# A two-block transformer on one core: TensorE's share of the background tasks tied to program order, longer pauses in two tasks, and the expert stage's first splits in another order

## The chip, the core and the metric

The kernel runs on one core of a Trainium2 chip. Five engines work side by side and synchronise by semaphores: TensorE (PE, matmuls; its weight loads are listed as PEld), VectorE (DVE), ScalarE (ACT), GpSimd (POOL) and SyncE (SP, which here only issues DMAs). Each engine runs its own instructions strictly in the order in which the program was laid out for it. The metric is the device time of one execution in microseconds (us); the median of the three runs of the kernel before is 2098.64 us.

## What is computed

The input is 256 tokens of 1024 channels. The first block is RMSNorm, a projection, three branches (windowed attention, a bidirectional gated linear recurrence after a short convolution, attention over a memory of 256 rows), a gated merge, and then a feed-forward over 16384 experts: every token scores 2 x 128 sub-keys in each of 8 heads, takes the top 16 of each half, combines them to 256 candidates, takes the top 16 again, and sums gate x gelu(u . h) x v over the chosen experts. Two more layers follow, each with four branches (retention, a convolution of 31 taps, a spatial gating unit, local attention with 8 heads in 2 groups over blocks of 128), a gated merge and a feed-forward.

```python
sc = jnp.einsum('bshpc,hpkc->bshpk', q, sub_keys)
top_v, top_i = lax.top_k(sc, PEER_TOPK)
...
best_v, best_pos = lax.top_k(cand_v, PEER_TOPK)
gate = jax.nn.softmax(best_v, axis=-1)
...
act = jax.nn.gelu(jnp.einsum('chkd,cd->chk', u_tab[ix], hx))
return jnp.einsum('chk,chkd->cd', gx * act, v_tab[ix])
```

The kernel does not gather. It multiplies all 16384 experts in 128 blocks of 128 ("u-blocks"), builds a dense gate for every token and expert from one-hot vectors, multiplies the two, and runs all of v as a second dense matmul.

## The kernel before, in words

**Weights as one stream.** All weights lie in DRAM as 5416 blocks of 128x128 in the order of their use. `Stream.blks` (line 101) hands out one block after the other; every eighth call opens a slot (`_slot`, line 77): ACT copies 128x1024 raw values into a rounded half `whi` (line 91), then DVE or POOL forms the rest `wlo` (line 94; POOL only during the expert projection and the top-k, where `pool_share` is (1, 1)). There are three slots (`SLOT_BUFS`), so ACT can be at most three slots of eight blocks ahead of PE. A matmul of fp32 quality is three matmuls (`mm3`, lines 172 to 176: whi with the high half of the activations, whi with the low half, wlo with the high half); `mm3a` (lines 178 to 182) does the same with 512 columns.

**Background tasks.** What lies between the large projections (attention, convolutions, top-k, the gates' one-hots) is written as generators. `add` (line 144) queues one, `tick` (line 154) is called once for every two weight blocks, and a task that yields n is resumed n x unit ticks later (unit is 4, but 1 for the top-k and the gates). `_step` (line 148) resumes a task, `finish` (line 164) runs it to its end at once. So the pauses are written in weight blocks, that is, in PE's main work.

**Who sets the order.** The program is written in one order, and a scheduler then lays out each engine's instructions (`TileContext(nc, schedule_with_timeline_sim=True)`). It follows the written order as priority, but takes another instruction first where its own timing model says that the first one's operands aren't there yet; so an instruction may stand earlier or later than it was written. The slots' instructions are written under `high_priority` and run ahead as far as their buffers allow. `with tc.issue_after(ins):` ties every instruction written inside, as far as it is on the engine of `ins`, to come after `ins`; the kernel has `ws.on_scalar` and `ws.on_vector`, the last `whi` on ACT and the last `wlo` on DVE.

**The expert stage** (`peer`, line 744). `topk` (line 932) adds the task `picks` (line 1021), then projects the queries (12 column blocks of 8 weight blocks each). `picks` runs eight units (`unit`, line 942), one for each pair of heads and each half of the tokens: PE scores (line 946), then DVE alone does top-16, candidates, top-16 again and index arithmetic with one-hots (lines 1056 to 1063, 953 to 989). A unit is started every `TK_PACE` = 22 ticks, but not before its queries exist. After the last one `yield TK_LAST` (20 ticks), then `gates` (line 991) for both halves, whose softmax has an exponential on ACT (line 997) between DVE's lines 996 and 998 to 1000; 6 ticks later `turn` (line 1004) transposes indices and gates on PE. Meanwhile `u_while` (line 771) multiplies u-blocks as long as the task lives. After that `build` (line 789) makes the gates of experts 0 to 63 of each row in 32 steps (`onehots` on DVE, lines 801 to 806; `products` on PE, ACT and DVE, lines 814 to 831), one step every 8 ticks, again under u-blocks. U-blocks that were made while their place was taken are merged afterwards by multiplications of 128x1024 (lines 853 to 857). A second `build` for experts 64 to 127 (`more`, one step every 10 ticks) is queued, the accumulators are taken, and the loop over v starts: eight weight blocks for each b, u-blocks that are still missing after every odd b, and `weighted` (line 862), which splits the product of gate and activation for b + 1 into `ga` on ACT and DVE (lines 187, 188). At b = 64 the task `more` must be finished (line 865). From block `done` on, `weighted` also has a DVE multiplication (line 868).

**Local attention** (`swa` in `mixers`, line 1221) has four groups in a layer. A group scores on PE (`pss`, line 1230), makes a softmax on DVE and ACT that ends with a multiplication on DVE (line 1247), pauses 3 (12 ticks), transposes on PE (`ptt`, line 244 called from 1255), pauses 1, and multiplies by v (line 1261). The groups are queued at distances of 3 (line 1295). The scores lie in `T4` tiles, of which a layer has 13; the tap convolution (line 1135) runs on DVE beside it, tied to `ws.on_vector`.

Of the kernel before, what the change touches and what calls it, by code (L numbers as in the profile page):

```python
# [7 lines left out]
F32 = mybir.dt.float32  # L8
# [4 lines left out]
AF = mybir.ActivationFunctionType  # L13
ALU = mybir.AluOpType
# [5 lines left out]
P = 128  # L20
S = 256
# [7 lines left out]
N_HA = 96  # L29
HALF = 64  # L30
TK_PACE = 22
TK_LAST = 20
T_OH = 8
PACE = {0: 7.5, HALF: 10}
G_SCALE = 4096.0
# [1 line left out]
NBLK = 128  # L37
# [6 lines left out]
N_BLOCKS = 5416  # L44
W_SHAPE = (-(-N_BLOCKS // 16), 128, 2048)
TAPS = 2
N_SCR = 5
LRU_PACE = 5
N_WARM = 50
# [81 lines left out]
class Core:  # L131
# [14 lines left out]
        return self.tasks[-1]  # L146

    def _step(self, t):
        try:
            t[1] = next(t[0]) * t[2]  # L150
        except StopIteration:
            self.tasks.remove(t)

    def tick(self):
        if self.ticking:
# [16 lines left out]
    def mm3(self, out, wh, wl, xh, xl, start, stop):  # L172
        mm = self.nc.tensor.matmul
        mm(out, lhsT=wh, rhs=xh, start=start, stop=False)  # L174
        mm(out, lhsT=wh, rhs=xl, start=False, stop=False)  # L175
        mm(out, lhsT=wl, rhs=xh, start=False, stop=stop)  # L176

    def mm3a(self, out, wh, wl, xh, xl, start, stop):
        mm = self.nc.tensor.matmul
        mm(out, lhsT=xh, rhs=wh, start=start, stop=False)  # L180
        mm(out, lhsT=xl, rhs=wh, start=False, stop=False)
        mm(out, lhsT=xh, rhs=wl, start=False, stop=stop)  # L182

    def split(self, hi, lo, src, scale=None, eng=None):
        nc = self.nc
# [177 lines left out]
    def build(self):  # L363
        tc, nc, a = self.tc, self.nc, self.a
        with ExitStack() as st:
            cp = st.enter_context(tc.tile_pool(name="cp", bufs=1))
            wp = st.enter_context(tc.tile_pool(name="wp", bufs=1))
            self.tp = st.enter_context(tc.tile_pool(name="tp", bufs=2))
            self.dr = st.enter_context(tc.tile_pool(name="dr", bufs=1, space=DRAM))
            self.cp = cp  # L370
            self.mm = st.enter_context(tc.tile_pool(name="mm", bufs=4, space=PSUM))
            self.bg = st.enter_context(tc.tile_pool(name="bg", bufs=4, space=PSUM))
            self.x = cp.tile([P, KD, S], F32, tag="x", name="x")
            self.par = cp.tile([P, P1_COLS + 2 * KD], F32, tag="par", name="par")
            self.cst = cp.tile([P, C_COLS], F32, tag="cst", name="cst")
            self.ws = Stream(self, wp, a["w"])
            with tc.high_priority(offset=2 * PRIO):
                nc.scalar.dma_start(out=self.par, in_=a["par1"])
                for k in range(0, KD, 2):
                    nc.sync.dma_start(out=self.x[:, k:k + 2, :], in_=a["xT"][:, k:k + 2, :])  # L380
                    if k < 4:
                        self.ws.first(4 * k)
                nc.scalar.dma_start(out=self.cst, in_=a["cst"])
            self.ident = self.cst[:, C_ID:C_ID + P]
            self.hh = cp.tile([P, KD, S], F32R, tag="hh", name="hh")
            self.hl = cp.tile([P, KD, S], F32R, tag="hl", name="hl")
            self.ones = cp.tile([P, 1], F32, tag="ones", name="ones")
            nc.vector.memset(self.ones, 1.0)
            self.eps = cp.tile([P, 1], F32, tag="eps", name="eps")
            nc.vector.memset(self.eps, EPS)  # L390
            self.sqrt_soon(self.eps)
            self.warm()
            self.block1()
            self.peer()
            for l in range(2):
                self.mixers(l)
                self.ffn(l)
# [346 lines left out]
    def peer(self):  # L744
# [4 lines left out]
        tc, nc, a, ws = self.tc, self.nc, self.a, self.ws  # L749
        with ExitStack() as st:  # L750
# [7 lines left out]
            ha = p.tile([P, N_HA, S], F32, tag="ha", name="ha")  # L758
            hb = None

            def h(b):
                return ha[:, b, :] if b < N_HA else hb[:, b - N_HA, :]
# [18 lines left out]
            with tc.tile_pool(name="peg", bufs=1) as gp:  # L781
# [63 lines left out]

                early = ahead
                u_while(self.add(build(0, early), unit=1), HALF + early, early)
                done = ahead
                assert done >= HALF

                cut = NBLK - N_HA
                for b0 in range(early, HALF, 4):
                    for b, k0, k1 in ((ha, b0, min(b0 + 4, HALF, cut)), (hb, max(b0, cut), min(b0 + 4, HALF))):
                        if k0 < k1:
                            o = HALF if b is ha else HALF - N_HA
                            nc.vector.tensor_tensor(out=ha[:, k0:k1, :], in0=ha[:, k0:k1, :],
                                                    in1=b[:, k0 + o:k1 + o, :], op=ALU.mult)
                more = self.add(build(HALF, done), unit=1)
                acc = [pool.tile([P, 2, S], F32, tag=t, name="acc")
                       for pool, t in ((self.mm, "mm"), (self.bg, "bg")) for _ in range(2)]  # L860

                def weighted(b, g):

                    if b == HALF:
                        self.finish(more)
                    src = h(b)
                    if b >= done:
                        nc.vector.tensor_tensor(out=src, in0=src, in1=h(b - done), op=ALU.mult)
                    self.split(g[:, 0, :], g[:, 1, :], src)
                    return g  # L870

                def v_cols(c, b, g, first, last):

# [1 line left out]
                    self.mm3(acc[c // 2][:, c % 2, :], wh, wl, g[:, 0, :], g[:, 1, :],  # L875
                             first and c % 2 == 0, last and c % 2 == 1)

                nxt = weighted(0, ga[0])
                for b in range(NBLK - LAST):
                    cur = nxt  # L880
                    if b + 1 < NBLK - LAST:
# [50 lines left out]
    def topk(self, tp, i1, i2, gt, iot):  # L932
# [58 lines left out]
        def gates(t):  # L991

            bv = bvs[t].rearrange("p (h k) -> p h k", k=16)
            e = tp.tile([P, 8, 16], F32, tag="ge", name="ge")
            sm = tp.tile([P, 2, 8], F32, tag="gs", name="gs")
            nc.vector.tensor_tensor(out=e, in0=bv, in1=bv[:, :, 0:1].to_broadcast([P, 8, 16]), op=ALU.subtract)
            nc.scalar.activation(out=e, in_=e, func=AF.Exp)
            nc.vector.tensor_reduce(out=sm[:, 0, :], in_=e, axis=AX.X, op=ALU.add)
            nc.vector.reciprocal(out=sm[:, 1, :], in_=sm[:, 0, :])
            nc.vector.scalar_tensor_tensor(out=slg[t].rearrange("p (h k) -> p h k", k=16), in0=e, scalar=G_SCALE,  # L1000
                                           in1=sm[:, 1, :, None].to_broadcast([P, 8, 16]),
                                           op0=ALU.mult, op1=ALU.mult)
# [63 lines left out]
    def mixers(self, l):  # L1066
        tc, nc, a, ws = self.tc, self.nc, self.a, self.ws
        with ExitStack() as st:
# [152 lines left out]
            def swa(n, g):  # L1221
# [19 lines left out]
                for i in range(4):  # L1241
# [4 lines left out]
                nc.vector.reciprocal(out=sm[:, 3, :], in_=sm[:, 1, :])  # L1246
                nc.vector.tensor_tensor(out=s[:, :, :nk], in0=s[:, :, :nk],
                                        in1=sm[:, 3, :, None].to_broadcast([P, 4, nk]), op=ALU.mult)
                yield 3
                nkb = nk // P  # L1250
                pts = []
                for kb in range(nkb):
# [39 lines left out]
            self.finish(*loads[1])  # L1292
            self.proj_b(W2["rq"](l), 2, KD, hh, hl, ev_rot(rq))
            self.finish(*t_qk, *loads[0])
            t_swa = [self.add(swa(n, g), 1 + 3 * (2 * n + g)) for n in range(2) for g in range(2)]
            self.proj_b(W2["rq"](l), 4, KD, hh, hl, ev_rot(rq), c0=2)
            self.proj_b(W2["rk"](l), 4, KD, hh, hl, ev_rot(rk))
            rv = T4().rearrange("p a b -> p (a b)").rearrange("p (t c) -> p t c", t=2)
# [326 lines left out]
```

## Time and profile before

| what | value |
|---|---|
| median of three runs | 2098.64 us (2097.73 to 2099.84) |
| the profiled execution's own time | 2103.45 us |
| its span, first to last instruction | 2101.7 us |
| mean granted TensorE clock | 0.986 |
| busy: PE, PEld, DVE, ACT, POOL | 2026.5, 1969.1, 1681.7, 1164.1, 254.8 us |
| instructions | 41465 |

The busy time of PE is 96% of the span, so the table alone says little; what matters is where PE stands, for whom, and at what clock it goes on afterwards. The page cuts the span into 40 slices of 52.5 us and gives each engine's busy share there in tenths. A list of waits sums, for each engine and line, how long it stood and which instruction released it. A timeline lists instructions with start, duration and, in brackets, the idle time before them. A table of stretches gives busy time, number of instructions, and the granted clock of TensorE (1.00 is 2.4 GHz, 0.50 is 1.2 GHz).

### The profile page before, as it was taken

The page shows a single profiled execution, that of the slowest core. Times are in us where ns is not written, and L with a number is a line of the kernel's source. Part 1 is how long each engine was busy: PE and PEld are TensorE (multiplying, and loading weights), DVE is VectorE, ACT ScalarE, POOL GpSimd, SP SyncE. Part 2 cuts the span into 40 slices and gives each one's busy share as a digit, 9 for nine tenths or more (in the row PEclk, how much of TensorE's full clock was granted, in tenths as well). Part 3 has the DMA queues.
Part 4 walks back from the last instruction along what each step waited for, and adds up shares of the span by engine and source line. Part 5 has one row for each costly group of instructions (what it writes and reads, how often), then busy time and mean ns, then how long its engine had stood idle before and what let it go on. Part 6 is the DMA issues. An engine that isn't in the chain of part 4 may idle for free.

```text
span 2101.7 us, 41465 instructions
## 1 busy us (share of the span) xinstructions
PE 2026.5 (96%) x16818; PEld 1969.1 (94%) x16818; DVE 1681.7 (80%) x3308; ACT 1164.1 (55%) x1910; POOL 254.8 (12%) x162
## 2 busy tenths in 40 slices
PE   8999999959999999999999989999999989999999
PEld 7989999959999999999999879999999979999997
DVE  7877779998999999995557989977555999977554
ACT  6688654435555455545546656466455656466443
POOL 2202208741000000000000101200000101200000
PEclk9999999979999999999999999999999999999999
DMA  5444554425454444445554633555555643554554
GB/s 210 141 131 167 209 207 181 161 100 182 181 177 169 157 167 175 172 159 193 201 187 175 219 140 140 182 188 194 193 190 199 219 161 121 201 184 180 193 187 150
DMA packets 57019, 370.01 MB, mean 176 GB/s; under 512 B 6587, under 2 KB 10236, under 8 KB 13564
## 3 DMA queue, kind: packets, MB, share of 16 engines
q1 hardware_dynamic: 50256, 357.06, 47.3%
q10 hardware_dynamic: 6572, 10.31, 1.7%
q8 instruction: 131, 2.15, 0.4%
q14 instruction: 60, 0.49, 0.1%
HBM read 364.73 MB, written 2.62 MB: 175 GB/s over the span
## 4 chain that ended last, share of the span: by engine, by line
PE 82%; DVE 8%; ACT 4%; issue 3%; DMA 2%; POOL 1%; ACTq 0%; SPq 0%; POOLq 0%; DVEq 0%
PE mm L176 6%; PE mm L175 6%; PE mm L174 6%; PE acc L175 6%; PE acc L174 5%; PE acc L176 5%; PE pu L174 5%; PE pu L175 5%; PE pu L176 5%; PE pg L176 3%; PE pg L174 3%; PE pg L175 3%; DVE wlo L94 2%; PE mm L182 2%; PE mm L180 2%
## 5 line engine op out<-in xcount | busy, mean ns | idle before, releaser
L91 ACT ACTIVATE whi<-raw 128x1024 fp32r<-128x1024 f32 x677 | 717.3, 1061 | 765.6 <-PE acc L175 173.5
L94 DVE TENSOR_TENSOR wlo<-raw,whi 128x1024 fp32r<-128x1024 f32 x629 | 779.3, 1239 | 319.5 <-ACT whi L91 314.4
L174 PE MATMUL pu<-hh,whi 128*128 128x256 f32 x1024 | 289.9, 283 | 22.8 <-ACT whi L91 22.8
L176 PE MATMUL mm<-hh,wlo 128*128 128x256 f32 x1008 | 282.8, 281 | 7.4 <-DVE wlo L94 7.4
L176 PE MATMUL pu<-hh,wlo 128*128 128x256 f32 x1024 | 286.7, 280 | 3.0 <-POOL wlo L94 3.0
L175 PE MATMUL pu<-hl,whi 128*128 128x256 f32 x1024 | 285.7, 279 | 0.0
L174 PE MATMUL mm<-hh,whi 128*128 128x256 f32 x1008 | 283.1, 281 | 0.0
L175 PE MATMUL mm<-hl,whi 128*128 128x256 f32 x1008 | 282.0, 280 | 0.0
L175 PE MATMUL acc<-ga,whi 128*128 128x256 f32 x1000 | 268.1, 280 | 3.9 <-DVE ga L188 3.9
L176 PE MATMUL acc<-ga,wlo 128*128 128x256 f32 x1000 | 267.6, 279 | 0.0
L174 PE MATMUL acc<-ga,whi 128*128 128x256 f32 x1000 | 242.3, 281 | 5.0 <-ACT ga L187 5.0
L174 PEld LDWEIGHTS pu<-hh,whi 128*128 128x128 f32 x1024 | 194.3, 190 | 23.0 <-ACT whi L91 23.0
L176 PEld LDWEIGHTS mm<-hh,wlo 128*128 128x128 f32 x1008 | 190.8, 189 | 10.3 <-DVE wlo L94 9.7
L174 PE MATMUL pg<-hh,whi 128*128 128x256 f32 x704 | 197.7, 281 | 0.7 <-ACT gth L618 0.7
L176 PE MATMUL pg<-hh,wlo 128*128 128x256 f32 x704 | 196.9, 280 | 1.1 <-DVE wlo L94 1.1
L176 PEld LDWEIGHTS pu<-hh,wlo 128*128 128x128 f32 x1024 | 193.9, 189 | 3.8 <-POOL wlo L94 3.7
L175 PE MATMUL pg<-hl,whi 128*128 128x256 f32 x704 | 196.1, 279 | 0.0
L175 PEld LDWEIGHTS pu<-hl,whi 128*128 128x128 f32 x1024 | 193.9, 189 | 0.0
L175 PEld LDWEIGHTS mm<-hl,whi 128*128 128x128 f32 x1008 | 192.0, 190 | 1.5 <-issue 1.3
L175 PEld LDWEIGHTS acc<-ga,whi 128*128 128x128 f32 x1000 | 188.8, 189 | 4.6 <-DVE ga L188 4.5
L174 PEld LDWEIGHTS mm<-hh,whi 128*128 128x128 f32 x1008 | 190.9, 189 | 1.0 <-issue 0.7
L176 PEld LDWEIGHTS acc<-ga,wlo 128*128 128x128 f32 x1000 | 188.7, 189 | 0.0
(412 smaller groups left out, 4866.2 us busy)
## 6 DMA issues: line engine op xcount, KB each, us to landing
raw<-in_w SPq DMA_DIRECT2D x336, 1024.0 KB
raw<-in_w SPq DMA_DIRECT2D x5, 512.0 KB
bias<-bias_scr ACTq DMA_DIRECT2D x4, 512.0 KB
bias_scr<-sbb ACTq DMA_DIRECT2D x16, 96.0 KB
cl<-in_cstl ACTq DMA_DIRECT2D x2, 576.0 KB
x<-in_xT SPq DMA_DIRECT2D x4, 256.0 KB
memt<-in_memT ACTq DMA_DIRECT2D x1, 1024.0 KB
keys<-in_keysT ACTq DMA_DIRECT2D x1, 1024.0 KB
```

Of the source, the lines that this page charges most:

```text
L91: self.on_scalar = nc.scalar.activation(out=hi, in_=src, func=AF.Copy).ins
L94: i = eng.tensor_tensor(out=lo, in0=src, in1=hi.bitcast(F32), op=ALU.subtract)
L174: mm(out, lhsT=wh, rhs=xh, start=start, stop=False)
L175: mm(out, lhsT=wh, rhs=xl, start=False, stop=False)
L176: mm(out, lhsT=wl, rhs=xh, start=False, stop=stop)
L180: mm(out, lhsT=xh, rhs=wh, start=start, stop=False)
L182: mm(out, lhsT=xh, rhs=wl, start=False, stop=stop)
```

## The change

- `_step` wraps every resumption of a background task in `issue_after(self.on_pe)`, where `on_pe` is the last matmul of the latest `mm3` or `mm3a`.
- `TK_LAST` goes from 20 to 48, and the exponential in `gates` is tied to come after `ws.on_scalar`.
- In local attention the pause before the transposes goes from 3 to 5, the distance of the groups from 3 to 4.
- At the border from u to v, the split for b = 0 is written first, then three u-blocks (`FILL`) with the merging multiplications spread over them and tied to `ws.on_vector`; the second `build` and the accumulators come after that. The multiplication in `weighted` is tied to `ws.on_vector` too.

```diff
-TK_LAST = 20
+TK_LAST = 48
+FILL = 3
+SWA_SOFT, SWA_PACE = 5, 4
...
     def _step(self, t):
-        try:
-            t[1] = next(t[0]) * t[2]
-        except StopIteration:
-            self.tasks.remove(t)
+        with self.tc.issue_after(self.on_pe):
+            try:
+                t[1] = next(t[0]) * t[2]
+            except StopIteration:
+                self.tasks.remove(t)
...
-        mm(out, lhsT=wl, rhs=xh, start=False, stop=stop)
+        self.on_pe = mm(out, lhsT=wl, rhs=xh, start=False, stop=stop).ins
...
-        mm(out, lhsT=xh, rhs=wl, start=False, stop=stop)
+        self.on_pe = mm(out, lhsT=xh, rhs=wl, start=False, stop=stop).ins
...
-                done = ahead
-                assert done >= HALF
-                cut = NBLK - N_HA
-                for b0 in range(early, HALF, 4):
...
-                            nc.vector.tensor_tensor(out=ha[:, k0:k1, :], in0=ha[:, k0:k1, :],
-                                                    in1=b[:, k0 + o:k1 + o, :], op=ALU.mult)
-                more = self.add(build(HALF, done), unit=1)
-                acc = [pool.tile([P, 2, S], F32, tag=t, name="acc")
-                       for pool, t in ((self.mm, "mm"), (self.bg, "bg")) for _ in range(2)]
+                assert ahead >= HALF
+                def collapse(b0):
...
+                            with tc.issue_after(ws.on_vector):
+                                nc.vector.tensor_tensor(out=ha[:, k0:k1, :], in0=ha[:, k0:k1, :],
+                                                        in1=b[:, k0 + o:k1 + o, :], op=ALU.mult)
...
                     if b >= done:
-                        nc.vector.tensor_tensor(out=src, in0=src, in1=h(b - done), op=ALU.mult)
+                        with tc.issue_after(ws.on_vector):
+                            nc.vector.tensor_tensor(out=src, in0=src, in1=h(b - done), op=ALU.mult)
...
+                done = NBLK
+                nxt = weighted(0, ga[0])
+                late = list(range(early, HALF, 4))
+                for i in range(FILL):
+                    for b in late[i * len(late) // FILL:(i + 1) * len(late) // FILL]:
+                        collapse(b)
+                    u_block(ahead, h(ahead))
+                    ahead += 1
+                done = ahead
+                more = self.add(build(HALF, done), unit=1)
+                acc = [pool.tile([P, 2, S], F32, tag=t, name="acc")
+                       for pool, t in ((self.mm, "mm"), (self.bg, "bg")) for _ in range(2)]
...
-                nxt = weighted(0, ga[0])
...
-            nc.scalar.activation(out=e, in_=e, func=AF.Exp)
+            with self.tc.issue_after(ws.on_scalar):
+                nc.scalar.activation(out=e, in_=e, func=AF.Exp)
...
-                yield 3
+                yield SWA_SOFT
...
-            t_swa = [self.add(swa(n, g), 1 + 3 * (2 * n + g)) for n in range(2) for g in range(2)]
+            t_swa = [self.add(swa(n, g), 1 + SWA_PACE * (2 * n + g)) for n in range(2) for g in range(2)]
```

## Rows read from the trace of the kernel before

**Rows 1.** The page: busy tenths in 40 slices, and TensorE's clock.
```profile
PE   8999999959999999999999989999999989999999
PEclk9999999979999999999999999999999999999999
```
**Rows 2.** Waits of PE, whole span: us in total, times, longest us.
```profile
PE pu L174 <- ACT whi L91: 22.8, 1, 22.8
PE ptt L244 <- DVE t L1247: 12.1, 4, 4.3
...
PE acc L174 <- ACT ga L187: 5.0, 1, 5.0
PE acc L175 <- DVE ga L188: 3.9, 2, 3.6
```
**Rows 3.** Timeline of ACT at the end of the top-k: start us, us, what.
```profile
410.26 0.37 ACT L769 ACTIVATE ha<-pu 128x256 f32<-128x256 f32 x1
...
439.44 0.31 ACT L997 ACTIVATE ge<-ge 128x128 f32<-128x128 f32 x1 [27.50 <-DVE ge L996]
```
**Rows 4.** Stretches, matmuls of u-blocks (tile pu) alone: PE, PEld, ACT busy, clock.
```profile
352.00:410.00 58.00, 56.95 (x482) 55.82 (x482) 7.30 (x20) 1.00 0.51 182
412.00:490.00 78.00, 51.43 (x417) 49.68 (x416) 6.36 (x17) 0.85 0.32 120
```
**Rows 5.** Stretches of whole top-k units: PE, PEld, DVE, ACT, POOL busy, clock.
```profile
358.00:382.00 24.00, 24.00 (x211) 24.00 (x210) 23.83 (x76) 10.69 (x17) 20.74 (x9) 1.00 0.50 180
382.00:404.30 22.30, 22.30 (x195) 22.30 (x194) 22.09 (x52) 10.37 (x16) 18.41 (x8) 1.00 0.51 186
419.00:431.00 12.00, 0.00 (x0) 0.00 (x0) 11.76 (x64) 0.00 (x0) 0.00 (x0) 0.63 0.00 1
```
**Rows 6.** Timeline of DVE, last two top-k units.
```profile
431.45 0.29 DVE L1059 MAX8 tv<-sc 128x8 f32<-128x128 f32 x1
...
439.12 0.28 DVE L996 TENSOR_TENSOR ge<-bv 128x128 f32<-128x128 f32 x1
...
459.43 0.28 DVE L996 TENSOR_TENSOR ge<-bv 128x128 f32<-128x128 f32 x1
...
469.45 0.69 DVE L989 TENSOR_REDUCE sl<-oh 128x32 f32<-128x512 f16 x1
```
**Rows 7.** Stretches just after two waits of PE, columns as in rows 5.
```profile
441.00:446.00 5.00, 3.36 (x15) 3.07 (x16) 5.00 (x4) 3.81 (x6) 4.71 (x3) 0.50 0.34 108
683.30:688.30 5.00, 5.00 (x27) 4.91 (x28) 5.00 (x5) 0.88 (x3) 0.00 (x0) 0.50 0.33 141
```
**Rows 8.** Stretches of local attention in the first layer, columns as in rows 5.
```profile
1190.00:1250.00 60.00, 51.44 (x359) 45.24 (x357) 57.99 (x103) 28.43 (x56) 7.36 (x4) 0.97 0.45 162
1250.00:1300.00 50.00, 49.34 (x331) 43.52 (x332) 40.97 (x99) 36.63 (x55) 1.85 (x1) 0.97 0.29 106
```
**Rows 9.** Timelines of PE and DVE, local attention, second and fourth group.
```profile
1208.54 0.72 PE L1230 MATMUL pss<-kT,t 64*128 64x128 f32 x8
...
1251.27 0.99 PE L1230 MATMUL pss<-kT,t 64*128 64x256 f32 x4
...
1229.95 0.69 DVE L1247 TENSOR_TENSOR t<-t,sm 128x512 f32<-128x512 f32 x1
...
1259.62 1.21 DVE L1247 TENSOR_TENSOR t<-t,sm 128x1024 f32<-128x1024 f32 x1
```
**Rows 10.** Timeline of DVE: a step of build, and the end of u.
```profile
654.34 0.69 DVE L801 TENSOR_TENSOR e<-iot,i 128x1024 f16<-128x1024 f16 x1 [0.35 <-PE pgb L814]
...
655.61 1.22 DVE L94 TENSOR_TENSOR wlo<-raw,whi 128x1024 fp32r<-128x1024 f32 x1
...
658.74 1.23 DVE L94 TENSOR_TENSOR wlo<-raw,whi 128x1024 fp32r<-128x1024 f32 x1
...
682.65 6.90 DVE L856 TENSOR_TENSOR ha<-ha,hb 128x1024 f32<-128x1024 f32 x6
...
927.94 3.44 DVE L868 TENSOR_TENSOR hb<-hb,ha 128x256 f32<-128x256 f32 x10
```

More of the change, by code (lines that the diff above doesn't have):

```diff
@@ L847, in peer @@
                 u_while(self.add(build(0, early), unit=1), HALF + early, early)
-                done = ahead
-                assert done >= HALF
-                cut = NBLK - N_HA
-                for b0 in range(early, HALF, 4):
-                    for b, k0, k1 in ((ha, b0, min(b0 + 4, HALF, cut)), (hb, max(b0, cut), min(b0 + 4, HALF))):
+                assert ahead >= HALF
+                def collapse(b0):
+                    cut = NBLK - N_HA
+                    b1 = min(b0 + 4, HALF)
+                    for b, k0, k1 in ((ha, b0, min(b1, cut)), (hb, max(b0, cut), b1)):
                         if k0 < k1:
                             o = HALF if b is ha else HALF - N_HA
-                            nc.vector.tensor_tensor(out=ha[:, k0:k1, :], in0=ha[:, k0:k1, :],
-                                                    in1=b[:, k0 + o:k1 + o, :], op=ALU.mult)
-                more = self.add(build(HALF, done), unit=1)
-                acc = [pool.tile([P, 2, S], F32, tag=t, name="acc")
-                       for pool, t in ((self.mm, "mm"), (self.bg, "bg")) for _ in range(2)]
+                            with tc.issue_after(ws.on_vector):
+                                nc.vector.tensor_tensor(out=ha[:, k0:k1, :], in0=ha[:, k0:k1, :],
+                                                        in1=b[:, k0 + o:k1 + o, :], op=ALU.mult)
                 def weighted(b, g):
```

## The prediction

> **What bounds the kernel now.** I read the page's slices first. PE is at nine tenths or more nearly everywhere; one slice falls to five tenths, and the next has the clock at seven [rows 1]. PE's waits, summed, name the places: 22.8 us once for `whi` in the u stage, 12.1 us in four waits for local attention's softmax, 5.0 us and 3.9 us for `ga` at the start and in the middle of v [rows 2]. These are 43.8 us, and the diff touches all four. The rest of the kernel is PE streaming weights, which the change leaves as it is.
>
> The largest wait is ACT's. Behind the gelu at 410.26 it stood 27.50 us before the exponential of `gates`, until DVE had delivered line 996 [rows 3]; each `whi` queued behind it, and PE ran dry. The exponential was written 15 u-blocks later, but the scheduler thought DVE further than it was and moved it up. DVE is late because POOL forms `wlo` beside it: a top-k unit takes 24.0 and 22.3 us with POOL busy, 12.0 us with POOL idle [rows 5]. A restart after such waits runs at half clock for some 5 us [rows 7].
>
> **The top-k's end.** What it loses now: 482 matmuls in 58 us is 2.89 us per u-block of 24; the 417 matmuls from 412 to 490 should take 50.2 us and take 78 [rows 4], so 27.8 us are lost, the wait, the slow clock and restarts together.
>
> What the change makes of it, in ticks: units start at 1, 23, ... 155, then 177, `TK_LAST`, `gates`, 6, `turn`, 4. `gates` goes from tick 197 to 225, the end from 207 to 235. The query projections take 48 ticks, a u-block 4, so `gates` goes from behind u-block 37 to behind u-block 44, and 47 instead of 40 u-blocks are made in the stage. The exponentials, tied to `on_scalar`, now come at the earliest behind the `whi` of the 44th u-block. That is written when the 41st is done (three slots), 18 u-blocks after the gelu at 410.26, the 23rd: 410.3 + 18 x 2.89 = 462.
>
> Is DVE ready then? At 404.3 a unit ended and four were left. With POOL always busy they take 4 x 23.1 us, to 497; line 996 of the last stands 10.7 us before its end [rows 6], so 486. PE has three u-blocks in hand and would stop at 470, POOL at 465, and from there DVE works at the 12-us rate: 9 us of the seventh unit, which shrink to 4.7, and 7.7 us to line 996 [rows 6] make 477. So **a wait is left**: PE stands from 470 to about 478.5, 8.5 us, then 1.6 us for the first `wlo` and 2.5 us for five at half clock, as after the old wait, where PE was busy 3.36 of the first 5 us at 0.50 [rows 7]. Next late is `turn`, whose transposes are now tied to PE's place in u-block 46: PE is there at about 487, DVE ends the last unit at 488 and then has lines 998 to 1000 twice, some 3 us. PE waits about 4 us more. Together 16 to 17 us are lost instead of 27.8: **gain 11**. Bounds: all 27.8 back if the scheduler sets the exponentials late enough; nothing if PE meets the wait for the full 486 and again at `turn`. I take 11, by the unit times, which are the nearest rows.
>
> The seven extra u-blocks are no extra work; they are missing later under v. Their `wlo` moves from DVE to POOL.
>
> **Border of u and v.** PE waits 5.0 us for the first `ga` while DVE runs the last gates and then six merges, 6.90 us [rows 2, 10], and goes on at half clock for five more [rows 7], another 2.4. The three `FILL` u-blocks, 8.7 us, now stand between the split and its use, and five merges instead of six are spread among them. They are not new work either. The cover is long enough: **gain 7 of 7.4**, between 4 and 8. If the merges held `wlo` up, that would be the next wait.
>
> **Middle of v.** The second wait for `ga` (3.9 us [rows 2]; with some 4 us at half clock 5.5) stands behind ten line-868 multiplications in one run, 3.44 us [rows 10], moved up by the scheduler. Tying them ends that, and there are 14 instead of 24. But the task `more` loses time: it steps every 10 ticks, 33 steps and the end, 331 ticks. Before, 63 b's and 24 u-blocks gave 348 ticks before b = 64; now 14 u-blocks are left (47 + 64 + 3 = 114 made), which gives 308. Two steps are forced at b = 64. One step is 4.4 us of DVE less a `wlo` of 1.2, 3.2 us [rows 10], and the second needs PE, ACT and DVE in turn; one b of PE work, 2.9 us, covers it. I expect 4 to 5 us of wait and the slow clock after it: **loss 1**, between a gain of 5 (the one-hots run ahead) and a loss of 5 (nothing does).
>
> **Local attention.** 12.1 us of waits, the longest 4.3 [rows 2], and clock 0.97 in the stretch [rows 8], which over 60 us is another 1.8 where PE works; both layers look alike, so up to 16. The longer pause is 8 ticks, 16 weight blocks or 5.8 us of PE time (2.89 us per eight), more than the longest wait. But DVE is busy 58.0 of 60 us there and 41.0 of 50 in the next stretch [rows 8]. Time that PE gains there must be found by moving DVE's work into the 9 us that are free later; the wider distance of the groups does that in part. The second group's scores now also come before the first one's transposes. **Gain 8**, between a loss (rival below) and 16.
>
> **Ties elsewhere.** An instruction that was moved up can only come later now; one that stood late stays. Nothing is added, no DMA is moved on SP or POOL. The ends of tasks are pauses away from their `finish`: local attention's last step moves from tick 56 to 76, while its branch begins 176 weight blocks or 88 ticks after the start. I cost this at nothing, within 3 us either way.
>
> **Sum.** 11 + 7 - 1 + 8 = 25 against the profiled execution's 2103.45 us (span 2101.7), which stands 4.8 us, 0.2%, above the median of 2098.64. So 2073.6 by the median; I round to **2073**.
>
> **Rivals.**
>
> *All of the top-k comes back*: DVE is further than I think, or the exponentials are placed later than the earliest place. For it: only the tie's lower end is known. Against: 23 us a unit, twice [rows 5]. 25 + 17 = 42 gained: 2057.
>
> *VectorE is the bound.* In these two stages DVE is busy 98% and 97% of the time [rows 5, 8], and a wait of PE that goes comes back as a wait for `wlo` or at the next transposes. Then the top-k gives 3, local attention nothing, the middle of v loses 3, the border gives 7: 7 gained, 2092. Against: in the u stage PE has other work to run ahead with. The Trainium skill's page Perfetto Trace Analysis, section Identifying the Most-Contended Engine, says that the engine with the highest occupancy is the one to work on, and its section Optimization Strategy that this engine can change with the regime; read so, this rival is its case. The trace agrees so far that DVE leads in both stretches.
>
> *Slower: the T4 ring.* At distance 4 the fourth group starts at tick 52, when 12 of 13 T4 tiles and the third group's scores are held, so it waits for the third's transposes at tick 56 and has 16 ticks, 11.6 us, to its own; `gu` queues behind it. The chain from scores to line 1247 took 8.4 us with DVE free and 21.4 us with DVE loaded [rows 9]. From 11.6 on PE stands: at 21.4, 10 us a layer and 2.5 for the clock, 25 in both. Without local attention's gain, 25 - 17 = 8 slower: 2107.
>
> *The change does nothing*: the scheduler had most of it in place and the new order brings equal waits; 2099.
>
> **Chances.** Forecast 0.48 (own range 2063 to 2083), all back 0.20, VectorE bound 0.20, slower 0.05, nothing 0.05, others 0.02. The range leaves out the last three and the edges: 2054 to 2094. About 0.2%, 4 us, is what a measurement of this kernel can tell from no change. Nearly all of the first three cases is faster by more: 0.88; within it 0.07; slower 0.05.
>
> **What would show it.** Right: in the new profile ACT's wait before line 997 is some 13 us instead of 27.5, PE's for `whi` about 8, and `ptk` has a wait of a few us; the 5.0 us for the first `ga` is gone; a wait for `ga` stays at b = 64 with `pgb` just before it; local attention's waits are about half. Wrong: no wait at the exponentials (2057), or new waits of PE for `wlo` in 1190 to 1250 (2092), or for `t` at the fourth group (2107).

## The result, and the profile after

The changed kernel takes 2077.26 us (median of four runs, 2066.51 to 2079.54) where the kernel before took 2098.18 us beside it (2092.68 to 2099.84). The ratio is 0.9888, 95% interval 0.9851 to 0.9925: faster by about 21 us. The profiled execution took 2076.68 us, span 2074.9 us, granted clock 0.994.

The page's slices of the changed kernel (busy tenths of PE, and TensorE's clock):

```profile
PE   8999999998999999999999999999999999999999
...
PEclk9999999999999999999999999999999999999999
```

The slice at five tenths and the clock at seven [rows 1] are gone. PE's waits over the whole span (us in total, times, longest):

```profile
PE acc L179 <- DVE ga L192: 10.0, 15, 1.1
PE pu L178 <- ACT whi L93: 6.7, 2, 6.0
PE mm L180 <- DVE wlo L96: 6.0, 4, 2.6
...
PE acc L178 <- ACT ga L191: 3.9, 1, 3.9
...
PE pu L180 <- POOL wlo L96: 1.8, 1, 1.8
```

Against [rows 2]: 22.8 us for `whi` became 6.7, the four waits for local attention's softmax are gone altogether, and so is the 5.0 us wait for the first `ga`. But a row has come in that was not there, ten us in fifteen small waits for `ga`. The timeline of ACT at the end of the top-k (start, duration, what, in brackets the idle time before):

```profile
468.13 0.31 ACT L1015 ACTIVATE ge<-ge 128x128 f32<-128x128 f32 x1
...
478.92 0.31 ACT L1015 ACTIVATE ge<-ge 128x128 f32<-128x128 f32 x1 [7.47 <-DVE ge L1013]
```

The wait of 27.50 us [rows 3] is now 7.47. PE's timeline there, and stretches of the expert stage (the first for tile `pu` alone, the second for all; columns as in [rows 4] and [rows 8]):

```profile
480.23 0.58 PE L178 MATMUL pu<-hh,whi 128*128 128x256 f32 x1 [6.02 <-ACT whi L93]
...
482.80 0.58 PE L180 MATMUL pu<-hh,wlo 128*128 128x256 f32 x1 [1.78 <-POOL wlo L96]
```

```profile
412.00:490.00 78.00, 68.71 (x557) 67.83 (x555) 8.82 (x24) 0.93 0.42 152
```

```profile
830.00:930.00 100.00, 91.89 (x819) 89.10 (x819) 87.53 (x205) 48.18 (x84) 0.00 (x0) 1.00 0.45 161
```

The 78 us hold 557 matmuls of u instead of 417 [rows 4]. At 2.89 us for 24 they should take 67.1, so 10.9 us are lost instead of 27.8. The 100 us of v hold 819 matmuls. The kernel before had 899 there and no waits, but it still had u-blocks to make up to 905 us, while the changed kernel's last one ends at 824.

**Where the time went, by stages.** The first `pn` matmul of each norm cuts the span. A second column is needed, because 256-column matmuls at full granted clock follow each other every 113.3 ns in some stretches and every 117.8 ns in others, in every kernel here, in a pattern that changes from profile to profile (last section). "Net" is the length less that excess: the sum, over the steps between 105 and 125 ns at full clock, of what is above 113.33 ns. It is worked out from the starts of all matmuls, and for each kernel from one profiled execution.

| stage | before, us | after, us | before, net | after, net | net change |
|---|---|---|---|---|---|
| up to the expert stage's norm (from the first `pn`) | 281.9 | 283.2 | 279.9 | 277.1 | -2.8 |
| expert stage | 843.2 | 835.2 | 831.8 | 822.5 | **-9.3** |
| mixers, first layer | 302.8 | 292.4 | 299.8 | 290.2 | **-9.6** |
| feed-forward, first layer | 180.6 | 180.6 | 180.5 | 180.5 | 0 |
| mixers, second layer | 292.8 | 287.7 | 290.7 | 285.6 | **-5.1** |
| last feed-forward | 182.7 | 177.8 | 178.7 | 177.5 | -1.2 |

The spans differ by 26.8 us, of which some 24 lie in the three stages that the change was about. The first and last rows are not the change's: experiments that leave that code alone have the shorter lengths too.

### The profile page after: what moved, and what is told of

The parts are those of the page before. It is cut to its first block, busy times and chain, and to the rows that moved or that the text cites. A ratio compares the mean times of both kernels' runs of the same rounds, so it can differ in the third digit from the quotient of the medians.

```text
span 2074.9 us, 41467 instructions
## 1 busy us (share of the span) xinstructions
PE 2022.9 (97%) x16818; PEld 1966.0 (95%) x16818; DVE 1680.6 (81%) x3290; ACT 1158.1 (56%) x1906; POOL 265.4 (13%) x169
## 4 chain that ended last, share of the span: by engine, by line
PE 69%; DVE 19%; ACT 2%; issue 2%; POOL 0%; ACTq 0%; DVEq 0%; POOLq 0%
PE mm L180 5%; PE mm L178 5%; PE mm L179 5%; PE acc L179 5%; PE acc L180 5%; PE acc L178 5%; PE pu L178 4%; PE pu L179 4%; PE pu L180 3%; PE pg L180 3%; PE pg L178 3%; PE pg L179 3%; DVE wlo L96 3%; PE pp L180 2%; PE pp L179 2%; PE pp L178 2%
## 5 line engine op out<-in xcount | busy, mean ns | idle before, releaser
L96 DVE TENSOR_TENSOR wlo<-raw,whi 128x1024 fp32r<-128x1024 f32 x622 | 769.1, 1237 | 299.4 <-ACT whi L93 297.6
L179 PE MATMUL acc<-ga,whi 128*128 128x256 f32 x1000 | 267.5, 281 | 10.0 <-DVE ga L192 10.0
L178 PE MATMUL acc<-ga,whi 128*128 128x256 f32 x1000 | 233.6, 280 | 3.9 <-ACT ga L191 3.9
```

The costliest lines, as they stand in the source:

```text
L96: i = eng.tensor_tensor(out=lo, in0=src, in1=hi.bitcast(F32), op=ALU.subtract)
```

## The experiments

All of them, with the expert stage's length, its excess and its net length, and the net length of the mixers (us, one profiled execution each):

| kernel | ratio to before (95%) | expert stage | excess | net | mixers 1, net | mixers 2, net |
|---|---|---|---|---|---|---|
| before | | 843.2 | 11.4 | 831.8 | 299.8 | 290.7 |
| after | 0.9888 (0.9851 to 0.9925) | 835.2 | 12.8 | 822.5 | 290.2 | 285.6 |
| e1, top-k's numbers alone | 0.9984 (0.9959 to 1.0009) | 846.0 | 11.9 | 834.1 | 296.2 | 291.9 |
| e2, both pauses alone | 0.9937 (0.9913 to 0.9962) | 853.7 | 19.6 | 834.1 | 291.1 | 285.3 |
| e3, order of the splits alone | 0.9974 (0.9942 to 1.0006) | 843.5 | 17.6 | 825.8 | 296.2 | 291.3 |
| e4, PE's tie alone | 0.9963 (0.9937 to 0.9989) | 836.3 | 6.2 | 830.1 | 298.8 | 290.5 |
| e5, after without PE's tie | 0.9896 (0.9867 to 0.9925) | 838.5 | 13.8 | 824.7 | 291.0 | 285.3 |
| e6, top-k's numbers and PE's tie | 0.9948 (0.9929 to 0.9967) | 844.2 | 15.5 | 828.7 | 301.5 | 293.0 |
| e7, after, u-blocks spread | 0.9843 (0.9821 to 0.9864) | 829.8 | 4.9 | 824.8 | 290.2 | 285.6 |
| e8, e7 with other numbers | 0.9821 (0.9800 to 0.9841) | 822.5 | 5.0 | 817.5 | 292.5 | 285.5 |
| e9, after, tie on `turn` only | 0.9850 (0.9819 to 0.9882) | 826.9 | 17.9 | 808.9 | 292.0 | 285.2 |
| e10, e9 with TK_LAST 68 | **0.9764** (0.9737 to 0.9792) | 814.6 | 8.1 | 806.5 | 291.9 | 285.4 |
| e11, longer pause alone | one run, 2091.42 us beside 2100.75 | 849.5 | 15.3 | 834.3 | 291.9 | 288.6 |
| e12, wider distance alone | one run, 2105.91 us beside 2100.75 | 846.7 | 12.4 | 834.3 | 302.6 | 291.3 |

Where the code of a stage is that of before (or, in the mixers, has PE's tie alone), its net length spreads by some 2.5 us (expert stage 831.8 to 834.3) or 5 us (first mixers 296.2 to 301.5). Less than that is no finding.

### e1: the top-k's two edits alone

```diff
-TK_LAST = 20
+TK_LAST = 48
...
-            nc.scalar.activation(out=e, in_=e, func=AF.Exp)
+            with self.tc.issue_after(ws.on_scalar):
+                nc.scalar.activation(out=e, in_=e, func=AF.Exp)
```

> The kernel before with TK_LAST 48 and the exponentials tied to on_scalar, nothing else. Theory (each stage's gain comes from its own edit): ACT's wait before the second exponential falls from 27.5 us to about 8, the top-k's end gains 14 us, and v pays for the 7 u-blocks that are made earlier: 17 instead of 24 are left, the waits for ga in the middle of v grow by 3 to 8 us. Sum 6 to 11 us faster than before, ratio 0.995 to 0.997; local attention and the border of u and v as before. Rival (PE's tie, the first item of the change, is what brings the gains): the long exponential wait stays near 27 us, or local attention's waits change here too, and the time is within 4 us of before.

Neither as a whole: the long wait of the exponential is gone, as the theory had it, but nothing was gained, as the rival had it. PE's waits, PE's timeline and ACT's timeline:

```profile
PE ptk L244 <- DVE sl L989: 23.2, 2, 21.3
```

```profile
449.93 0.47 PE L244 MATMUL ptk<-cst,sl 128*128 128x128 f32 x1 [21.32 <-DVE sl L989]
```

```profile
454.35 1.06 ACT L91 ACTIVATE whi<-raw 128x1024 fp32r<-128x1024 f32 x1 [24.68 <-PE pu L175]
```

The scheduler moved the first transpose of `turn` ahead of some fifteen u-blocks, and PE stood for the one-hot sums of a top-k unit as it had stood for `whi` before. ACT now waits for PE, not for DVE. The same wait has come through another instruction. The local-attention waits (11.7 us) stayed, against the rival.

### e2, e11, e12: local attention's two numbers, together and one by one

```diff
-                yield 3
+                yield 5
...
-            t_swa = [self.add(swa(n, g), 1 + 3 * (2 * n + g)) for n in range(2) for g in range(2)]
+            t_swa = [self.add(swa(n, g), 1 + 4 * (2 * n + g)) for n in range(2) for g in range(2)]
```

e2 has both hunks, e11 the first, e12 the second.

> The kernel before with the softmax pause 5 instead of 3 and the groups 4 instead of 3 apart, nothing else. Theory: the pauses alone make all of local attention's gain; PE's waits for the four softmax tiles (12.1 us before) are gone, both mixer stages together are 14 to 17 us shorter, ratio 0.992 to 0.9935; the expert stage keeps its 27.5 us wait. Rival (PE's tie is needed for it): some of the waits for the softmax tiles stay, and the gain is under 8 us, ratio over 0.996.

> The kernel before with the softmax pause 5 instead of 3, the groups 3 apart as before. Theory (the pause between scores and transposes decides): PE's waits for the four softmax tiles, 12 us before, fall below 3 us, both mixer stages together are 9 us or more shorter. Rival (the distance of the groups decides, since it is what spreads VectorE's work): 6 us or more of these waits stay.

> The kernel before with the groups 4 instead of 3 apart, the softmax pause 3 as before. Theory (the pause decides): 6 us or more of the 12 us of waits for the softmax tiles stay. Rival (the distance decides): they fall below 3 us.

With both, PE's waits have no row for `ptt` left, and the mixers have the net lengths of the changed kernel: 6 to 7 us less in each layer than the mean of the five profiles with both old numbers (298.5 and 291.5 us; before, e1, e3, e4, e6), and ratio 0.9937. So PE's tie isn't needed here. The pause alone does most of it: no row for `ptt` either, and 9.5 us less in both layers; 2 us come back as a wait for `po`. The distance alone does nothing but shift the waits; e12's row of PE's waits:

```profile
PE ptt L244 <- DVE t L1247: 10.7, 2, 6.6
```

Two waits instead of four, but longer. What it adds to the longer pause, 4 us over both layers by one profile each, is not clear of the spread.

### e3: the order of the splits alone

The change less PE's tie, with `TK_LAST` 20, the exponentials untied and the pauses 3 and 3.

> The kernel before with the new order of the expert stage's splits (FILL, collapse, first weighted split ahead, the DVE ties), without PE's tie, without the new TK_LAST, exponential tie and pauses. Theory: the wait of 5.0 us for the first ga and its slow clock go (gain 6), 21 u-blocks are left under v instead of 24, so that the middle of v keeps its waits near the 5.5 us of before or a little more; sum 3 to 8 us faster, ratio 0.996 to 0.9985. Rival (the loss in the middle of v in the changed kernel comes from the DVE ties on the multiplications, not from the missing u-blocks): the middle of v shows ten or more waits of about 0.9 us here too, and the kernel is 4 to 6 us slower than before.

PE's only row of waits for `ga` in e3:

```profile
PE acc L177 <- DVE ga L190: 2.9, 2, 2.6
```

The border's wait fell from 5.0 to 2.6 us, and in the middle of v none is left, though 21 u-blocks stand there instead of 24. The expert stage is 6.0 to 8.5 us shorter, net. So the ties on VectorE alone do not make the small waits of the changed kernel.

### e4: PE's tie alone

```diff
     def _step(self, t):
-        try:
-            t[1] = next(t[0]) * t[2]
-        except StopIteration:
-            self.tasks.remove(t)
...
+        with self.tc.issue_after(self.on_pe):
+            try:
+                t[1] = next(t[0]) * t[2]
...
-        mm(out, lhsT=wl, rhs=xh, start=False, stop=stop)
+        self.on_pe = mm(out, lhsT=wl, rhs=xh, start=False, stop=stop).ins
...
-        mm(out, lhsT=xh, rhs=wl, start=False, stop=stop)
+        self.on_pe = mm(out, lhsT=xh, rhs=wl, start=False, stop=stop).ins
```

> The kernel before with PE's tie on the steps of background tasks alone. Theory: no instruction that bounds anything moves; within 3 us of before, ratio 0.9985 to 1.0015, the four waits for the softmax tiles and the 27.5 us exponential wait stay. Rival (PE's tie makes the gains, the numbers little): 8 us or more faster, ratio below 0.996, and the waits for the softmax tiles shrink.

Between the two: faster by 2 to 13 us. PE's waits:

```profile
PE pu L176 <- ACT whi L91: 17.2, 1, 17.2
PE ptt L246 <- DVE t L1249: 11.7, 4, 4.3
...
PE acc L177 <- DVE ga L190: 5.0, 4, 3.8
```

The softmax waits stay, as the theory had it; but the wait for `whi` is 17.2 instead of 22.8 us, and the stage is 2 to 4 us shorter, net, which is hardly clear of the spread. Of the four waits for `ga`, the 3.8 us are the old one in the middle of v, and only two small ones, 0.4 and 0.2 us, stand before it: with all 24 u-blocks left, the tie alone does not bring the changed kernel's series of waits. This profile also has the least excess of the kernels with the old numbers, 11.1 us over the whole span against 22.9; how much of the timed gain is that stays open.

### e5: the changed kernel without PE's tie

> The changed kernel without PE's tie on the steps of background tasks. Theory (PE's tie is worth little alone, but the top-k's gain needs it): as in the run with the top-k's numbers alone, the transposes of sl move ahead of u-blocks and PE stands some 20 us before them, the expert stage is 9 to 17 us longer than in the changed kernel, local attention keeps its whole gain; ratio to before 0.992 to 0.997. Rival (TK_LAST and the exponential's tie do it by themselves, the earlier run was a chance of the scheduler's): no wait over 10 us before the transposes, ratio within 0.003 of 0.989.

The ratio is the rival's, 0.9896, but the place is the theory's: the transposes were moved up again, and PE stands 21.4 us for them. But net the stage is only 2.2 us longer than the changed kernel's, not 9 to 17. PE's waits:

```profile
PE ptk L246 <- DVE sl L1004: 23.0, 2, 21.4
...
PE acc L177 <- DVE ga L190: 2.2, 3, 1.1
```

What the theory lacked is the second row. Without the tie the waits for `ga` fall from 13.9 to 2.2 us, and none of those is in the middle of v. The stretch from 830 to 930 us (us, then PE, PEld, DVE, ACT, POOL busy, clock):

```profile
830.00:930.00 100.00, 98.72 (x868) 95.06 (x867) 99.02 (x245) 50.61 (x92) 0.00 (x0) 1.00 0.47 165
```

DVE is busy 99.0 of 100 us here, and 87.5 in the changed kernel, which has the waits. So DVE is not too slow there; it is made to stand. DVE's own waits for PE in that stretch, first in the changed kernel, then in e5:

```profile
DVE e L805 <- PE pgb L818: 12.5, 12, 1.7
```

```profile
DVE e L803 <- PE pgb L816: 0.4, 1, 0.4
```

Two timelines of DVE show it, first the changed kernel, then e5:

```profile
849.19 0.41 DVE L192 TENSOR_TENSOR ga<-ha,ga 128x256 fp32r<-128x256 f32 x1
851.25 0.69 DVE L805 TENSOR_TENSOR e<-iot,i 128x1024 f16<-128x1024 f16 x1 [1.65 <-PE pgb L818]
851.86 0.75 DVE L810 TENSOR_TENSOR e1g<-e,gt 128x512 f16<-128x512 f16 x2
852.54 1.22 DVE L96 TENSOR_TENSOR wlo<-raw,whi 128x1024 fp32r<-128x1024 f32 x1
...
857.35 0.42 DVE L192 TENSOR_TENSOR ga<-ha,ga 128x256 fp32r<-128x256 f32 x1
```

```profile
846.80 0.42 DVE L190 TENSOR_TENSOR ga<-ha,ga 128x256 fp32r<-128x256 f32 x1
847.27 0.69 DVE L803 TENSOR_TENSOR e<-iot,i 128x1024 f16<-128x1024 f16 x1
847.88 0.42 DVE L808 TENSOR_TENSOR e1g<-e,gt 128x512 f16<-128x512 f16 x1
```

And PE in the changed kernel:

```profile
850.59 0.63 PE L818 MATMUL pgb<-e1g,e 128*128 128x128 f16 x8
...
857.83 0.39 PE L179 MATMUL acc<-ga,whi 128*128 128x256 f32 x1 [0.63 <-DVE ga L192]
...
859.09 0.63 PE L818 MATMUL pgb<-e1g,e 128*128 128x128 f16 x8
```

With the tie the eight matmuls of a one-hot step stand at their written place, and the next one-hots, which need their buffer, hold DVE for 1.65 us behind them (about 1.65 and 0.45 us in turn from step to step); the `ga` at 857.35 comes 0.63 us after PE wanted it. The steps stand 8.1 to 8.5 us apart, and thirteen such waits stand between 830 and 932 us. In e5 they come every 6.5 us, ahead of their pace, the eight matmuls often in two halves, and the last at 930.4 us: nothing is left to force at b = 64.

The tie is not the whole condition. In the three kernels that have it on all steps and make a u-block after every second b, the series of waits begins where the u-blocks end: the last u-block stands at 824 us and the first small wait at 831 in the changed kernel, at 844 and 854 in e6 (17 u-blocks left), at 893 and 900 in e4 (24 left).

### e6: the top-k's edits with PE's tie

> The kernel before with TK_LAST 48, the exponentials' tie and PE's tie; pauses and the order of the expert stage's splits as before. Theory: the long wait is replaced as in the changed kernel by one of 6 to 8 us at the second exponential, under 1 us at the transposes of slg; 12 to 15 us come back there, 3 to 8 us of it are lost again in the middle of v (17 u-blocks left instead of 24); ratio 0.994 to 0.997, local attention as before. Rival (the top-k needs the new order of the splits too): a wait over 15 us is left in the top-k's end, ratio over 0.997.

As the theory had it, but for 1.3 us at the transposes of `slg`. PE's waits:

```profile
PE ptt L246 <- DVE t L1250: 11.9, 4, 4.3
PE acc L177 <- DVE ga L190: 10.8, 12, 4.9
PE pu L176 <- ACT whi L91: 7.6, 1, 7.6
```

No long wait is left at the top-k's end, where e1 had 21.3 us, and the waits for `ga` are back in v, in a kernel without the new order of the splits. The top-k's edits gain only with the tie, and the tie with fewer u-blocks left brings its own loss along.

### e7: the remaining u-blocks spread over v

```diff
-                    if b % 2 and ahead < NBLK:
+                    if b % 4 == 3 and ahead < NBLK:
```

> The changed kernel with the 14 u-blocks that are left put after every fourth b of v instead of every second, so that they last until b = 55. Theory (VectorE's load in the part of v without u-blocks makes the waits): the ten waits of about 1 us for ga in the middle of v go, the one of 4 us at b = 64 stays, the expert stage is 6 to 10 us shorter than in the changed kernel, ratio to before 0.983 to 0.986. Rival (the ties on VectorE's multiplications make these waits, whatever the load): waits of about 1 us for ga stay, ten or more, and the stage is within 3 us of the changed kernel's.

The ratio fell into the range, but not for the reason given. PE's waits:

```profile
PE acc L179 <- DVE ga L192: 7.9, 16, 2.3
...
PE acc L178 <- ACT ga L191: 3.9, 1, 3.9
```

Sixteen waits are left, 7.9 us instead of 10.0, the one of 3.9 us at b = 64 stands as it did, and net the stage is 2.3 us longer than in the changed kernel. What is shorter in the profile is its excess, 4.9 instead of 12.8 us. So VectorE's load by itself does not make these waits: with the load spread and the tie kept they stay, and with the load as it was and the tie taken off (e5) they go. The load has a part in their size: the waits in the middle of v are 0.3 to 0.5 us here, with u-blocks among them, and 0.4 to 0.75 in the changed kernel, without.

### e8: later exponentials, spread u-blocks, a shorter pause of the one-hots

```diff
-TK_LAST = 48
+TK_LAST = 60
-PACE = {0: 7.5, HALF: 10}
+PACE = {0: 7.5, HALF: 9}
-                    if b % 2 and ahead < NBLK:
+                    if b % 5 == 4 and ahead < NBLK:
```

> The changed kernel with TK_LAST 60 instead of 48, the u-blocks left under v (11 then) after every fifth b, and the one-hot task's pause in v 9 instead of 10 ticks. Theory: the exponentials come three u-blocks later, so that the wait of 7.5 us before the second one, 2 us of restart and the slow clock after it go or shrink to 2 us; in the middle of v the 1-us waits go and at most one step of the one-hot task is left at b = 64; the expert stage is 15 to 24 us shorter than in the changed kernel, ratio to before 0.977 to 0.983. Rival (VectorE is the bound of the stage as a whole): what is saved at the top-k's end is lost again under v, and the ratio stays within 0.003 of 0.989.

Half of it, though the ratio is in the range. The wait at b = 64 went, but 8.1 us in eighteen small waits for `ga` stayed, and PE still stood 4.3 us for `whi`. Net the stage is 5.0 us shorter than the changed kernel's, not 15; the rest of the ratio is excess (5.0 us against 12.8).

### e9 and e10: the tie where it is needed, and then the exponentials later

```diff
     def _step(self, t):
-        with self.tc.issue_after(self.on_pe):
-            try:
-                t[1] = next(t[0]) * t[2]
...
-            for t in range(2):
-                turn(t)
+            with self.tc.issue_after(self.on_pe):
+                for t in range(2):
+                    turn(t)
```

e10 also has `TK_LAST` 68.

> The changed kernel with PE's tie taken off the steps of all tasks and put around the top-k's turn alone. Theory (the tie is needed for the transposes of the top-k and harmful in the middle of v, where it keeps the scheduler from running the one-hots ahead): at the top-k's end the waits are those of the changed kernel (6 to 8 us before u, about 2 us after it, under 1 us at the transposes), in the middle of v there are none over 0.6 us between 830 us and 935 us and none of 4 us at b = 64; net of the matmul step the expert stage is 9 to 15 us shorter than in the changed kernel, ratio to before 0.980 to 0.985. Rival (the tie works through other steps, the units' or the one-hots', and not through turn): PE waits 15 us or more before the transposes again, ratio 0.988 or more.

> The same with TK_LAST 68 instead of 48: five u-blocks later, so 9 instead of 14 are left under v. Theory: the wait before the second exponential (7.5 us of ACT, 6 us of PE) goes or is under 1 us, with the restart and most of the slow clock behind it; the one-hot task has less room under v, up to 4 us of waits come back at b = 64; 3 to 9 us faster than the kernel with the tie around turn alone, ratio to before 0.977 to 0.982. Rival (v then lacks the u-blocks): waits in v of 8 us or more, no faster than with 48.

e9's waits of PE:

```profile
PE pu L176 <- ACT whi L93: 6.0, 1, 6.0
...
PE acc L177 <- DVE ga L190: 1.6, 3, 1.2
```

The top-k's end has the waits of the changed kernel, v those of e5, and the stage is 13.6 us shorter than the changed kernel's, net. The timed ratio, 0.985, only touches the forecast's edge: this profile has the most excess of all, 29.9 us over the span, and the timed interval still overlaps the changed kernel's. That the tie on `turn` is enough for the top-k's end, and that the waits in v need the tie on the other steps, is shown by this run with e5. That it is the one-hots' step among them is read from the timelines; no run ties it alone. e10's waits:

```profile
PE pu L178 <- POOL wlo L96: 3.0, 2, 2.1
PE ptk L246 <- DVE slg L1016: 2.8, 1, 2.8
```

No row for `pu` behind `whi` is left, the second exponential waits 1.28 us, and the stage has no stretch at half clock (34.1 us of them before, 13.7 after). With nine u-blocks left v still has no wait over 0.6 us, so the rival falls. It is 14.7 us faster than e9, more than expected; net its stage is only 2.4 us shorter, within the spread, and 13.1 us of the two profiles' difference of 15.0 are excess (29.9 against 16.8). At 2054.26 us, against 2100.75 for the kernel before beside it, this version is faster than both: its interval lies wholly below the changed kernel's.

## Why the prediction was right, and where its steps were not

The total was forecast at 2073 us and came at 2077; the gain of 25 us by the text stands against 21 timed and 26.8 between the two profiled spans. It is made of terms that were off in both directions: the top-k's end and local attention gave some 6 us more each, the middle of v 10 less. That the total came so close is in part luck.

- **The top-k's end: +11 forecast, +17 measured** (27.8 lost before, 10.9 after). DVE's line before the exponential was forecast ready at 477 and came at 478.6; PE was forecast to stand from 470 to 478.5, and stood from 474.2 to 480.2; the first exponential came at 468.1, not at the earliest place of 462. The 4 us at `turn` were 0.5: DVE had ended the unit when PE got there. Shown by e1, e5 and e6: this term needs PE's tie. The text saw that the transposes were tied, but counted it as a cost and put nothing on what happens without it: 21 us.
- **Border of u and v: +7 forecast, some +6 measured**: before, 5.0 us of wait and up to 3.4 of slow clock; after, 2.1 us of waits at full clock. e3 shows that it needs none of the other edits.
- **The middle of v: -1 forecast, -11 measured. This is the step that failed.** Thirteen small waits came that no sentence foresaw, 10.7 us by the starts of PE's matmuls, beside the one at b = 64, which came as forecast (3.9 us for `ga`, with `pgb` just before). With 1.7 us for 3.4 us at half clock that makes some 16 us lost, against 5.5 before. The step said that the ties on line 868 end the old wait and that two forced steps replace it, "between a gain of 5 (the one-hots run ahead) and a loss of 5 (nothing does)". Without PE's tie it is the upper end (e5, e9); with the tie it is below the lower one, because where no u-blocks are left a one-hot step that can't move holds DVE behind PE's matmuls. With all 24 u-blocks left (e4) the tie costs about 1 us there, so the two edits that were costed apart, the tie and the 10 u-blocks fewer, make this loss together. The paragraph on ties elsewhere, "I cost this at nothing, within 3 us either way", is where it was mis-sized: the tie was costed only for the ends of tasks, not for the tasks that could run ahead once the u-blocks are done.
- **Local attention: +8 forecast, 13 to 15 measured.** The two profiles give 14.7, net; the means over all kernels with the old and the new numbers 7 and 6 us. That DVE would have to make room took off half in the forecast, but with the longer pause little came in its place: 12.1 us of waits for the softmax went, and those for `wlo` in both mixers rose from 3.7 to 5.4 us. The stretches of [rows 8] in the changed kernel:

```profile
1190.00:1250.00 60.00, 57.76 (x376) 49.26 (x375) 57.80 (x103) 37.30 (x73) 5.57 (x3) 1.00 0.42 157
1250.00:1300.00 50.00, 49.36 (x405) 47.23 (x404) 49.74 (x112) 27.86 (x41) 7.01 (x4) 1.00 0.41 149
```

DVE is busy 49.74 of the second 50 us, 40.97 before. The slack was there to be used.

- The terms of the expert stage, 17, 6 and -11, make 12 where its net length changed by 9.3; the other 3 us are not placed.

So the title's first item, the tie of all tasks, nets about nothing in this kernel. Net of the excess, its part at `turn` saves 15.8 us (e5 to e9) and its part at all other steps costs 13.6 (e9 to the changed kernel), which is why e5, without it, is about as fast.

**The rivals.** "VectorE is the bound" fell: of the waits that went only the 1.7 us for `wlo` came back in the mixers, and in the middle of v, where waits came, DVE was less busy. The prediction also read [rows 5] wrongly for it: in the two top-k units with POOL busy PE leads, 24.00 us of 24.00 and 22.30 of 22.30, and DVE has 23.83 and 22.09; DVE leads in [rows 8]. The Trainium skill's page Perfetto Trace Analysis, section Identifying the Most-Contended Engine, would have the engine with the highest occupancy worked on first. In the middle of v DVE's share would mislead: it is 87.5% with the waits and 99.0% without them, by the same work done earlier. Its next step, in the section Optimization Strategy, to look at that engine's gaps and what ends them, does lead to the place: the 12.5 us of DVE behind `pgb`. The T4 ring's wait did not come; the fourth group's transposes have none.

## What to carry to other kernels

A wait that is tied away on one engine comes back on the next engine whose instruction the scheduler may still move up (e1), so tie the whole step, but only the step that was in the way: a tie over all background tasks also stops those that profitably run ahead. Judge a stage that is busy by who waits inside it, not by its busy share; in the middle of v DVE at 99.0% was running ahead, and at 87.5% it held PE up. Slack that another edit uses up (here the u-blocks left under v) can turn a tie that costs little (e4) into one that costs much (the changed kernel). Where two stages of a change pull in opposite directions, compare stage by stage; the total can look right for the wrong reasons.

## What the runs showed of the chip

Unexpected was that the matmul step has two values at granted clock 1.00. The feed-forward stage after the first mixers is the same work in all fourteen profiles and takes 180.6 us in thirteen, and 187.3 us in e9. The same stretch of e9, then of e10 (PE, PEld, DVE, ACT, POOL busy, clock, DMA share, GB/s):

```profile
1520.00:1560.00 40.00, 40.00 (x342) 40.00 (x341) 21.06 (x26) 18.31 (x25) 0.00 (x0) 1.00 0.52 185
```

```profile
1520.00:1560.00 40.00, 40.00 (x356) 40.00 (x355) 22.46 (x28) 18.61 (x24) 0.00 (x0) 1.00 0.52 187
```

342 matmuls against 356, with PE busy throughout, the clock at 1.00, and DMA share and VectorE's load alike: 117.8 ns a step against 113.3, from the beginning of the stage to its end. Per profile the excess adds up to 10.6 to 29.9 us, which is as wide as the spread of a kernel's own times here (the kernel before from 2094.83 to 2112.93 us beside e1 to e4). What switches it no row shows, and the timed runs beside the profiled ones have no such figure. It is why the text compares net lengths: by raw length e7, 5.4 us shorter than the changed kernel in that stage, would have looked like a gain.
